# FoX scores: the second score matmul contracts 128 rows instead of 64, with the low parts of the queries repeated in both halves

## The chip, the cores and the metric

One core of one Trainium2 chip runs the whole kernel. The metric is the device time of one execution in microseconds (us); lower is better. The kernel before took 1130.22 us, the median of three runs (1130.16 to 1131.38).

## The reference, cut to what matters

One residual layer on 1024 tokens of width 1024: a normalised projection, two mixers beside each other (HGRN2 with four heads, FoX with eight heads of width 64), an output projection, a mixture of 16 experts, a final norm. The change is in FoX, which is softmax attention with a decay bias, in blocks of 128 queries:

```python
logits = jnp.einsum('bhtd,bhsd->bhts', qb, k) + (cb[..., :, None] - cum[..., None, :])
mask = (start + jnp.arange(Q_BLOCK))[:, None] >= key_pos[None, :]
logits = jnp.where(mask, logits, NEG_INF)
p = jax.nn.softmax(logits, axis=-1)
return jnp.einsum('bhts,bhsd->bhtd', p, v)
```

The inputs are float32, and the kernel keeps their accuracy by splitting a value into a high part in the type float32r and a low part, the rest.

## The kernel before, in words

The head of the kernel (about 0 to 590 us) holds the projections, HGRN2 and FoX; then come the output projection with the router (to about 740 us) and the experts. The order in which the parts are written is at lines 563 to 587: `hg_v`, `hg_fq`, `hg_core` are HGRN2, `fox_v`, `fox_gate`, `fox_kq`, `fox_core` are FoX, `hg_g` a gate projection. A planner in the build (`schedule_with_timeline_sim`) takes this order as a priority and fixes the order of each engine's instructions; each engine then runs its list strictly in order, and waits where an input is late. So attention of one pair of heads and projections or HGRN2 steps of others stand mixed in TensorE's list. The fourth pair is advanced by hand (`next(steps)`, lines 585 and 655 to 694), with pieces of the output projection (`front_a`, `front_parts`, `prep`) between its steps.

**fox_kq(p)**, line 287, makes the queries and keys of heads 2p and 2p+1. A projection (`proj_c`, lines 248 to 255, through `mm3`, lines 243 to 246: three matmuls of 128 rows and 512 columns for each of 8 slices, twice) leaves the two heads in the two halves of 128 partitions. `ev_k` and `ev_q` split it: `ka` and `kl` are the high and low parts of the keys, `qa` and `ql` those of the queries. Then copies inside the on-chip memory (`mv`, line 285, on the SP queue) arrange them: for the first head `ka` becomes high parts over low parts, and `qa` its high parts twice; `kb` and `qb` are the same for the second head. The result is a pair of operand pairs for each head.

**row(i, hh)**, line 347, makes the logits of query block i, in chunks of at most 512 keys. Each chunk is two matmuls into one PSUM bank (lines 363 and 364). The first has 128 rows: high queries twice against high and low keys. The second has 64 rows: low queries against high keys. VectorE then adds the bias and takes the minimum (lines 367 and 372), ScalarE takes the exponential (line 375). `Gt` and `Gd` are the bias tiles, made by GpSimd (lines 353 to 355). **attend** (line 378) transposes the result (line 388), splits it (lines 393, 394) and multiplies by the values (lines 398, 399); **collect** and **finish** gather the output. There are 4 pairs, 2 heads each, and 4 x 1 + 4 x 2 = 12 chunks for each head, so 96 pairs of score matmuls.

Tiles come from rotating tags: "u" (15 slots of 4 KB per partition, for all of q, k, v and the HGRN2 tiles), "L" (4 slots, for the logits of a row and others), "Gd" (3 slots). A tile that finds no free slot waits until one is released. `front_a(1)`, line 611, loads a gate tile `gm` from a pool of its own. HGRN2's score matmuls (line 491) write 64 columns of the array.

Of the kernel before, what the change touches and what calls it, by code (L numbers as in the profile page):

```python
# [7 lines left out]
F32 = mybir.dt.float32  # L8
# [11 lines left out]
NT = S // 128  # L20
# [8 lines left out]
NSLOT = E * CAP  # L29
NROW = NSLOT + NOV * 128  # L30
EPS = 1e-6
NU = 15
NWARM = 14
BIG = 1.0e30
NEG = 3.0e38
# [45 lines left out]
def build(ctx, tc, x, attn_norm, w_in, hg_lb_logits, hg_norm, fox_f_bias, fox_norm, w_out, ffn_norm,  # L81
          w_group, b_group, w_expert, b_expert, w_gate, w_up, w_down, final_norm, cf, ci, cl0, out, dbg=None):
# [8 lines left out]
    cst = ctx.enter_context(tc.tile_pool(name="cst", bufs=1))  # L91
# [56 lines left out]
    up = up_cm.__enter__()  # L148
# [6 lines left out]
    def rtile(name):  # L155
        return up.tile([128, S], F32R, name=name, tag="u", bufs=NU)

    def ltile(name):
        return up.tile([128, S], F32, name=name, tag="L", bufs=4)
# [18 lines left out]
        return hi, lo  # L178

    XT, HV0 = [], []  # L180
    xst = cst.tile([128, NT, 5], F32, name="xst")
    warm = ltile("warm")[:, 0:128]
    V.memset(warm, 0.0)
    b = rbank()
# [99 lines left out]
    def mv(d, o):  # L284
        nc.sync.dma_start(d.bitcast(F32), o.bitcast(F32))

    def fox_kq(p):
        ka, kb, qa, qb, ql = (rtile(n) for n in ("ka", "kb", "qa", "qb", "ql"))
        kl = up.tile([128, S], F32R, name="kl", tag="L", bufs=4)

        def ev_k(b, sl):
            A.copy(ka[:, sl], b)
            V.tensor_sub(kl[:, sl], b, ka[:, sl].bitcast(F32))  # L293

        def ev_q(b, sl):
            A.activation(qa[:, sl], b, AF.Copy, scale=-0.125)
            V.scalar_tensor_tensor(ql[:, sl], b, -0.125, qa[:, sl].bitcast(F32), op0=OP.mult, op1=OP.subtract)
        proj_c(2560 + 128 * p, ev_k)
        mv(kb[64:128], ka[64:128])
        mv(kb[0:64], kl[64:128])  # L300
        mv(ka[64:128], kl[0:64])
        proj_c(2048 + 128 * p, ev_q)
        mv(qb[64:128], qa[64:128])
        mv(qb[0:64], qa[64:128])
        mv(qa[64:128], qa[0:64])
        out = (((qa, ka), (ql[0:64], ka[0:64])), ((qb, kb), (ql[64:128], kb[64:128])))
        FS[p] = out

    cld = dr.tile([64, 128], F32, name="cld")
# [1 line left out]
    def fox_gate():  # L311
        zt = ltile("zt")[:, 0:256].rearrange("p (a b) -> p a b", a=4)
        ffv = ff.rearrange("p h i -> p (h i)")
        V.tensor_scalar(zt[:, 0], ffv, 0.0, None, op0=OP.min)
        V.scalar_tensor_tensor(zt[:, 1], ffv, -1.0, ffv, op0=OP.mult, op1=OP.max)
        A.activation(zt[:, 2], zt[:, 1], AF.Exp, scale=-1.0)
        A.activation(zt[:, 2], zt[:, 2], AF.Ln, bias=1.0)
        V.tensor_sub(zt[:, 3], zt[:, 0], zt[:, 2])
        b = cbank()
        T.matmul(b[:, 0:64], tri, zt[:, 3], start=True, stop=True)  # L320
        cl = up.tile([128, 128], F32, name="cl", tag="Gd", bufs=3)[:, 0:64]
        V.tensor_copy(cl, b[:, 0:64])
        b = cbank()
        T.transpose(b[0:64, 0:128], cl, ident)
        clT = up.tile([128, 128], F32, name="clT", tag="Gd", bufs=3)[0:64]
        V.tensor_copy(clT, b[0:64, 0:128])
        nc.sync.dma_start(cld, clT)

    cdv = cld.rearrange("r s -> (r s)")
    fls = cst.tile([128, 4, 5, 8, 2], F32, name="fls")  # L330

    LF = {}

    def fox_steps(p):
        Gt, ntot = [], []
        for hh in range(2):
            h = 2 * p + hh
# [3 lines left out]
            V.tensor_scalar(n_, g_[:, :, 127], -1.0, None, op0=OP.mult)  # L341
            Gt.append(g_)
            ntot.append(n_)
        fl = fls[:, p]
        OS = otile("OF")

        def row(i, hh):
            nb = i + 1
            (q1, k1), (q2, k2) = FS[p][hh]
            qi = slice(i * 128, (i + 1) * 128)  # L350
            gv = Gt[hh].rearrange("p i s -> p (i s)")
            Gd = up.tile([128, 128], F32, name="Gd", tag="Gd", bufs=3)
            G.tensor_add(Gd, Gt[hh][:, i], msk)
            if i:
                G.tensor_scalar(Gt[hh][:, 0:i], Gt[hh][:, 0:i], 1.0, ntot[hh][:, i - 1:i], op0=OP.mult, op1=OP.add)  # L355
            L = ltile("Lg")
            mn = up.tile([128, 4], F32, name="mn", tag="mn", bufs=6)
            prev = 3.0e38
            k = 0
            for c0 in range(0, nb * 128, 512):  # L360
                c1 = min(nb * 128, c0 + 512)
                b = rbank()
                T.matmul(b[:, :c1 - c0], q1[:, qi], k1[:, c0:c1], start=True, stop=False)
                T.matmul(b[:, :c1 - c0], q2[:, qi], k2[:, c0:c1], start=False, stop=True)
                e = min(c1, i * 128)
                if e > c0:
                    V.tensor_tensor_reduce(L[:, c0:e], b[:, :e - c0], gv[:, c0:e], scale=1.0, scalar=prev,  # L367
                                           op0=OP.add, op1=OP.min, accum_out=mn[:, k:k + 1])
                    prev = mn[:, k:k + 1]
                    k += 1  # L370
                if c1 == nb * 128:
                    V.tensor_tensor_reduce(L[:, e:c1], b[:, e - c0:c1 - c0], Gd, scale=1.0, scalar=prev,
                                           op0=OP.add, op1=OP.min, accum_out=mn[:, k:k + 1])
                    prev = mn[:, k:k + 1]
            A.activation(L[:, :nb * 128], L[:, :nb * 128], AF.Exp, scale=-1.0, bias=prev, accum_out=fl[:, 0, i, hh:hh + 1])
            return L
# [97 lines left out]
        proj_c(512 + 128 * h, ev_f)  # L474
        proj_c(128 * h, ev_q)

    hgs = cst.tile([128, 4, 4, NT], F32, name="hgs")

    def hg_core(h):
        Fh, Kh, Qh, VV = HF[h], HK[h], HQ[h], HV[h]  # L480
        sct = up.tile([128, S], F32, name="sc", tag="sc", bufs=1).rearrange("p (c t) -> p c t", c=NT)
        sc = [sct[:, 0:4], sct[:, 4:8]]

# [12 lines left out]
        for li, hs in enumerate(LEVELS):  # L496
# [8 lines left out]
            n = S // (2 * hs)  # L505
# [8 lines left out]
        for half in range(2):  # L514
            bk = hbank()
            for c in range(4):
                s_ = slice((half * 4 + c) * 128, (half * 4 + c + 1) * 128)
                T.transpose(bk[:, c * 128:(c + 1) * 128], Kh[:, s_], ident)
            kt = Kh[:, half * 512:half * 512 + 512]
            A.copy(kt, bk)  # L520
            bv = hbank()
            nn = 4 if half == 0 else 3
            for c in range(nn):
                cc = half * 4 + c
                T.matmul(bv[:, c * 128:(c + 1) * 128], kt[:, c * 128:(c + 1) * 128], VV[:, cc * 128:(cc + 1) * 128],
                         start=True, stop=True)
            for c in range(nn):
                cc = half * 4 + c
                s_ = up.tile([128, 128], F32, name="st", tag="st", bufs=4)
                if cc == 0:  # L530
                    V.tensor_copy(s_, bv[:, 0:128])
                else:
                    V.scalar_tensor_tensor(s_, st[cc], Fh[:, cc * 128 + 127:cc * 128 + 128],
                                           bv[:, c * 128:(c + 1) * 128], op0=OP.mult, op1=OP.add)
                st[cc + 1 if cc < NT - 1 else 0] = s_
            bo = hbank()
            for c in range(4):
                cc = half * 4 + c
                cs = slice(c * 128, c * 128 + 128)
                v = VV[:, cc * 128:(cc + 1) * 128]  # L540
                T.matmul(bo[:, cs], sc[half][:, c], v, start=True, stop=cc == 0)
                if cc:
                    T.matmul(bo[:, cs], Qh[:, cc * 128:(cc + 1) * 128], st[cc], start=False, stop=True)
            isl = slice(half * 4, half * 4 + 4)
            A.copy(sc[half], bo.rearrange("p (c v) -> p c v", c=4))
            sq = Qh[:, half * 512:half * 512 + 512].rearrange("p (i v) -> p i v", i=4)
            G.tensor_mul(sq, sc[half], sc[half])
            st_ = hgs[:, h, :, 4 * half:4 * half + 4]
            V.tensor_reduce(st_[:, 0], sq, axis=AX.X, op=OP.add)
            V.tensor_scalar(st_[:, 0], st_[:, 0], 1.0 / 128, EPS, op0=OP.mult, op1=OP.add)  # L550
            rsqrt(st_[:, 1], st_[:, 0], st_[:, 2], st_[:, 3])
            G.tensor_mul(sc[half], sc[half], st_[:, 1, :, None].to_broadcast([128, 4, 128]))
            nc.sync.dma_start(o_d[512 * half:512 * half + 512, 128 * h:128 * h + 128].rearrange("(i t) c -> t i c", t=128), sc[half])
# [57 lines left out]
    def front_a(i):  # L611
        om = oa.tile([128, D], F32, name="om")
        if i < 1:
            HE[i] = oa.tile([128, D], F32, name="he", bufs=1)
        gm = HE[i][:, 0:512] if i in HE else (hp[0] if hp else oa).tile([128, 512], F32, name="gm", bufs=1)
        nc.sync.dma_start(om, o_d[i * 128:(i + 1) * 128, :])
        nc.sync.dma_start(gm, g_d[i * 128:(i + 1) * 128, :])
        V.tensor_mul(om[:, 0:512], om[:, 0:512], gm)
# [708 lines left out]
```

## Time and profile before

| | |
|---|---|
| median of three runs | 1130.22 us |
| span of the profiled execution, first to last instruction | 1129.1 us (its own time is not listed apart) |
| TensorE matmul busy | 1070.2 us, 95% of the span |
| VectorE, ScalarE, GpSimd busy | 61%, 47%, 38% |
| score matmuls (lines 363 and 364) | 192, in 96 pairs, from 140 to 584 us |

Times in the trace are in us from the span's start. Matmuls are pipelined and their ends are modelled, so the distance from one start to the next is the better measure of what one costs. PE is TensorE's matmul, PEld its weight load, DVE VectorE, ACT ScalarE, POOL GpSimd, SP the engine that issues most transfers. "64\*128" in a row of PE is the shape of the loaded weights, 64 rows by 128 columns. "issue" as a releaser means that the engine waited for nothing that the profile shows.

### The profile page before, as it was taken

The page shows a single profiled execution, that of the slowest core. Times are in us where ns is not written, and L with a number is a line of the kernel's source. Part 1 is how long each engine was busy: PE and PEld are TensorE (multiplying, and loading weights), DVE is VectorE, ACT ScalarE, POOL GpSimd, SP SyncE. Part 2 cuts the span into 40 slices and gives each one's busy share as a digit, 9 for nine tenths or more (in the row PEclk, how much of TensorE's full clock was granted, in tenths as well). Part 3 has the DMA queues.
Part 4 walks back from the last instruction along what each step waited for, and adds up shares of the span by engine and source line. Part 5 has one row for each costly group of instructions (what it writes and reads, how often), then busy time and mean ns, then how long its engine had stood idle before and what let it go on. Part 6 is the DMA issues. An engine that isn't in the chain of part 4 may idle for free. (4 is left out here: it accounts for less than half of the span.)

```text
span 1129.1 us, 19387 instructions
## 1 busy us (share of the span) xinstructions
PE 1070.2 (95%) x7405; PEld 881.9 (78%) x7405; DVE 684.5 (61%) x1674; ACT 536.3 (47%) x884; POOL 428.9 (38%) x382
## 2 busy tenths in 40 slices
PE   7999999999999999889989999699999999999993
PEld 7988877788879877778967888576777778778791
DVE  5446346664677238843484576656777777778363
ACT  6423264423443264325671242465666767667241
POOL 2023244433352136422261232444655555555213
PEclk8999999999999999998999999799999999999997
DMA  7211510222111411161135952379999999999973
GB/s 240 54 42 39 141 47 19 66 66 57 39 48 44 116 38 29 48 212 68 43 117 154 397 184 94 99 242 373 370 308 319 364 325 360 318 319 376 298 262 134
DMA packets 102048, 193.98 MB, mean 172 GB/s; under 512 B 9468, under 2 KB 43372, under 8 KB 101952
## 3 DMA queue, kind: packets, MB, share of 16 engines
q1 hardware_dynamic: 90656, 169.97, 43.0%
q0 software_dynamic: 7568, 20.96, 7.5%
q10 hardware_dynamic: 3728, 1.77, 0.7%
q8 instruction: 60, 0.98, 0.4%
q14 instruction: 36, 0.29, 0.1%
HBM read 155.85 MB, written 30.68 MB: 165 GB/s over the span
## 5 line engine op out<-in xcount | busy, mean ns | idle before, releaser
L244 PE MATMUL bk<-whi,xhi 128*128 128x256 f32 (+1 forms) x384 | 113.9, 296 | 2.3 <-ACT xhi L212 1.8
L245 PE MATMUL bk<-wlo,xhi 128*128 128x256 f32 (+1 forms) x384 | 112.5, 293 | 0.7 <-DVE wlo L177 0.7
L246 PE MATMUL bk<-whi,xlo 128*128 128x256 f32 (+1 forms) x384 | 112.2, 292 | 0.0
L1029 DVE TENSOR_TENSOR wl<-we,wh 128x1024 fp32r<-128x1024 f32 x64 | 92.0, 1448 | 33.2 <-ACT wh L1027 32.2
L1027 ACT CAST wh<-wm 128x1024 fp32r<-128x1024 f32 x84 | 87.2, 1049 | 48.3 <-PE ch L246 45.4
L245 PE MATMUL ch<-wl,xh 128*128 128x512 f32 (+1 forms) x336 | 108.1, 322 | 0.0
L244 PE MATMUL ch<-wh,xh 128*128 128x512 f32 (+1 forms) x336 | 107.2, 326 | 0.0
L246 PE MATMUL ch<-wh,xl 128*128 128x512 f32 (+1 forms) x336 | 107.1, 320 | 0.0
L1027 ACT CAST wh<-we 128x1024 fp32r<-128x1024 f32 x84 | 87.2, 1049 | 38.4 <-PE ch L246 38.2
L244 PE MATMUL bk<-xhi,whi 128*128 128x512 f32 x256 | 103.2, 403 | 1.7 <-DVE kl L293 1.2
L1029 DVE TENSOR_TENSOR wl<-wm,wh 128x1024 fp32r<-128x1024 f32 x63 | 93.5, 1515 | 17.0 <-ACT wh L1027 17.0
L245 PE MATMUL bk<-xlo,whi 128*128 128x512 f32 x256 | 102.5, 400 | 0.0
L246 PE MATMUL bk<-xhi,wlo 128*128 128x512 f32 x256 | 101.6, 397 | 0.0
L355 POOL TENSOR_SCALAR Gt<-Gt,ntot 128x128 f32<-128x128 f32 (+6 forms) x56 | 44.6, 796 | 91.8 <-DVE mn L367 82.1
L393 ACT CAST ph<-ch 128x512 fp32r<-128x512 f32 (+1 forms) x80 | 42.8, 542 | 76.8 <-PE ch L388 76.7
L244 PEld LDWEIGHTS bk<-whi,xhi 128*128 128x128 f32 x384 | 75.5, 196 | 4.9 <-ACT xhi L212 2.4
L1029 POOL TENSOR_TENSOR wl<-we,wh 128x1024 fp32r<-128x1024 f32 x20 | 51.1, 2554 | 69.8 <-ACT wh L1027 69.8
L245 PEld LDWEIGHTS bk<-wlo,xhi 128*128 128x128 f32 x384 | 75.2, 196 | 2.3 <-DVE wlo L177 1.2
L246 PEld LDWEIGHTS bk<-whi,xlo 128*128 128x128 f32 x384 | 75.1, 196 | 1.6 <-issue 0.9
L1029 POOL TENSOR_TENSOR wl<-wm,wh 128x1024 fp32r<-128x1024 f32 x21 | 52.4, 2493 | 53.2 <-ACT wh L1027 53.2
L245 PEld LDWEIGHTS ch<-wl,xh 128*128 128x128 f32 x336 | 64.0, 190 | 9.0 <-issue 4.1
L244 PEld LDWEIGHTS ch<-wh,xh 128*128 128x128 f32 x336 | 63.4, 190 | 7.8 <-ACT xh L1041 1.6
(413 smaller groups left out, 2719.6 us busy)
## 6 DMA issues: line engine op xcount, KB each, us to landing
we<-in_w_gate_dram SPq DMA_DIRECT2D x8, 2048.0 KB
we<-in_w_up_dram SPq DMA_DIRECT2D x8, 2048.0 KB, 18.2
we<-in_w_down_dram SPq DMA_DIRECT2D x8, 2048.0 KB, 15.7
wm<-in_w_gate_dram SPq DMA_DIRECT2D x8, 2048.0 KB, 8.5
wm<-in_w_up_dram SPq DMA_DIRECT2D x8, 2048.0 KB
wm<-in_w_down_dram SPq DMA_DIRECT2D x8, 2048.0 KB, 14.1
wraw<-in_w_in_dram SPq DMA_DIRECT2D x26, 512.0 KB, 4.2
xt<-in_x_dram SPq DMA_DIRECT2D x8, 512.0 KB, 11.6
```

Source lines behind the costliest of these rows:

```text
L244: T.matmul(o, l[0], r[0], start=first, stop=False)
L245: T.matmul(o, l[0], r[1], start=False, stop=False)
L246: T.matmul(o, l[1], r[0], start=False, stop=last)
L355: G.tensor_scalar(Gt[hh][:, 0:i], Gt[hh][:, 0:i], 1.0, ntot[hh][:, i - 1:i], op0=OP.mult, op1=OP.add)
L393: LF['act'] = A.copy(ph[:, :o], b[:, :o])
L1027: A.copy(hi, src)
L1029: (G if j % 3 == 2 else V).tensor_sub(lo, src, hi.bitcast(F32))
```

## The change

The low parts of the queries get the layout that the high parts have. `ql` becomes the first head's low parts in both halves, and a new tile `qm` holds the second head's in both halves; three more copies make them, the third of which overwrites a part that the first two read. The second score matmul takes whole tiles, so it contracts 128 rows, and adds the product of the low queries and the low keys. Space for the new tile: "u" has 16 slots; "Gd" has 2; the small tiles `xst`, `fls`, `hgs` move into rotating tags; `gm` of `front_a(1)` takes a slot of "L".

```diff
-NU = 15
+NU = 16
...
-    xst = cst.tile([128, NT, 5], F32, name="xst")
+    xst = up.tile([128, NT, 5], F32, name="xst", tag="sg", bufs=2)
...
-        ka, kb, qa, qb, ql = (rtile(n) for n in ("ka", "kb", "qa", "qb", "ql"))
+        ka, kb, qa, qb, ql, qm = (rtile(n) for n in ("ka", "kb", "qa", "qb", "ql", "qm"))
...
         mv(qb[64:128], qa[64:128])
         mv(qb[0:64], qa[64:128])
         mv(qa[64:128], qa[0:64])
-        out = (((qa, ka), (ql[0:64], ka[0:64])), ((qb, kb), (ql[64:128], kb[64:128])))
+        mv(qm[64:128], ql[64:128])
+        mv(qm[0:64], ql[64:128])
+        mv(ql[64:128], ql[0:64])
+        out = (((qa, ka), (ql, ka)), ((qb, kb), (qm, kb)))
...
-        cl = up.tile([128, 128], F32, name="cl", tag="Gd", bufs=3)[:, 0:64]
+        cl = up.tile([128, 128], F32, name="cl", tag="Gd", bufs=2)[:, 0:64]
...
-    fls = cst.tile([128, 4, 5, 8, 2], F32, name="fls")
...
-        fl = fls[:, p]
+        fl = up.tile([128, 5, 8, 2], F32, name="fls", tag="fls", bufs=2)
...
-            Gd = up.tile([128, 128], F32, name="Gd", tag="Gd", bufs=3)
+            Gd = up.tile([128, 128], F32, name="Gd", tag="Gd", bufs=2)
...
-    hgs = cst.tile([128, 4, 4, NT], F32, name="hgs")
...
+        hgs = up.tile([128, 4, NT], F32, name="hgs", tag="hgs", bufs=2)
...
-            st_ = hgs[:, h, :, 4 * half:4 * half + 4]
+            st_ = hgs[:, :, 4 * half:4 * half + 4]
...
-        gm = HE[i][:, 0:512] if i in HE else (hp[0] if hp else oa).tile([128, 512], F32, name="gm", bufs=1)
+        gm = HE[i][:, 0:512] if i in HE else hp[0].tile([128, 512], F32, name="gm", bufs=1) if hp else ltile("gm")[:, 0:512]
```

## Rows read from the trace of the kernel before

**Rows 1.** Windows, attention stages: length; busy PE, PEld, DVE, ACT, POOL; clock; DMA share; GB/s

```profile
135.00:225.00 90.00, 89.88 (x565) 66.91 (x564) 49.79 (x143) 47.85 (x75) 38.37 (x50) 1.00 0.19 54
262.00:330.00 68.00, 67.41 (x568) 54.90 (x567) 43.82 (x142) 26.95 (x72) 28.17 (x39) 1.00 0.13 37
393.00:462.00 69.00, 66.33 (x490) 48.31 (x488) 44.00 (x125) 33.17 (x60) 33.03 (x43) 1.00 0.13 36
504.00:590.00 86.00, 78.50 (x500) 67.33 (x501) 47.11 (x137) 56.48 (x93) 32.80 (x33) 0.92 0.28 94
```

**Rows 2.** TensorE's timeline around one pair of score matmuls: start, duration, line, tiles, shape

```profile
419.62 0.40 PE L363 MATMUL rb<-ka,qa 128*128 128x512 f32 x1
419.95 0.50 PE L364 MATMUL rb<-ka,ql 64*128 64x512 f32 x1
420.38 0.50 PE L245 MATMUL bk<-xlo,whi 128*128 128x512 f32 x1
420.72 0.39 PE L246 MATMUL bk<-xhi,wlo 128*128 128x512 f32 x1
420.95 0.39 PE L244 MATMUL bk<-xhi,whi 128*128 128x512 f32 x1
```

**Rows 3.** TensorE's weight loads in the same stretch, by timeline

```profile
419.95 0.18 PEld L364 LDWEIGHTS rb<-ka,ql 64*128 64x128 f32 x1 [0.37 <-issue]
420.38 0.19 PEld L245 LDWEIGHTS bk<-xlo,whi 128*128 128x128 f32 x1 [0.25 <-issue]
...
420.72 0.19 PEld L244 LDWEIGHTS bk<-xhi,whi 128*128 128x128 f32 x1
```

**Rows 4.** TensorE's timeline at smaller widths, and at the lines 491 and 388

```profile
262.40 0.28 PE L245 MATMUL bk<-wlo,xhi 128*128 128x256 f32 x1
262.52 0.28 PE L246 MATMUL bk<-whi,xlo 128*128 128x256 f32 x1
262.73 0.34 PE L491 MATMUL hc<-hQ,hK 128*64 128x64 f32 x4
...
147.33 0.38 PE L364 MATMUL rb<-kb,ql 64*128 64x256 f32 x1
147.64 0.44 PE L388 MATMUL ch<-cft,Lg 128*128 128x128 f32 x2
147.83 0.48 PE L244 MATMUL bk<-xhi,whi 128*128 128x512 f32 x1
```

**Rows 5.** SP's issues of query copies of pairs 0 to 2, and output weights, by timeline

```profile
132.58 2.08 SPq L285 DMA_DIRECT2D qb<-qa  x2
134.76 0.53 SPq L172 DMA_DIRECT2D wraw<-in_w_in_dram  x1
137.55 0.46 SPq L285 DMA_DIRECT2D qa<-qa  x1
...
261.31 0.47 SPq L285 DMA_DIRECT2D qa<-qa  x1
...
389.97 0.46 SPq L285 DMA_DIRECT2D qa<-qa  x1
...
493.37 2.51 SPq L592 DMA_DIRECT2D woraw<-in_w_out_dram  x3
```

**Rows 6.** Time from issue to landing of the copies into qb, by tile

```profile
DMA to landing us min/median/max: 2.9/3.6/3.7
```

**Rows 7.** TensorE's timeline: the first L364 of pairs 0, 1 and 2

```profile
140.91 0.32 PE L364 MATMUL rb<-ka,ql 64*128 64x128 f32 x1
...
264.55 0.33 PE L364 MATMUL rb<-ka,ql 64*128 64x128 f32 x1
...
395.68 0.33 PE L364 MATMUL rb<-ka,ql 64*128 64x128 f32 x1
```

**Rows 8.** Waits of the fourth attention stage: who, for whom, total us, times, longest

```profile
PE bk L624 <- DVE om L618: 1.8, 1, 1.8
PE rb L363 <- DMA qa<-qa: 1.7, 1, 1.7
```

More of the change, by code (lines that the diff above doesn't have):

```diff
@@ L324, in fox_gate @@
         T.transpose(b[0:64, 0:128], cl, ident)
-        clT = up.tile([128, 128], F32, name="clT", tag="Gd", bufs=3)[0:64]
+        clT = up.tile([128, 128], F32, name="clT", tag="Gd", bufs=2)[0:64]
         V.tensor_copy(clT, b[0:64, 0:128])
```

## The prediction

> **What bounds the kernel now.** I read three views. First the windows over the four stretches in which attention runs [rows 1]: TensorE is busy for 89.88 of 90 us, 67.41 of 68, 66.33 of 69 and 78.50 of 86, while VectorE, the next, has 49.79 of 90 and 47.11 of 86. So TensorE sets the pace in the first two stages, nearly so in the third, and in the fourth most of the time. A busy TensorE can still be held up inside, so the second view is its timeline, read by distances between starts [rows 2]. Ordinary matmuls of 512 columns stand 0.23 us apart (420.72 to 420.95). Around a 64-row score matmul the distances are 0.33 (419.62 to 419.95), 0.43 (to 420.38) and 0.34 us (to 420.72). Three ordinary ones would take 0.70 us; these take 1.10. The third view, the weight loads [rows 3], says why: in the ordinary stream a load starts while the matmul before it runs (L244's load at 420.72, its matmul at 420.95). The load of the 64-row matmul starts only together with that matmul, after 0.37 us without a load, and the load of the 128-row matmul behind it is late too (0.25 us). Going from 128 rows to 64 and back stops the loading ahead, twice for each pair.
>
> **Part 1, the wider matmul.** The same 96 matmuls remain, with the same columns and the same weight columns; only the rows grow. An L364 of 128 rows has the form of L363, so I price it as an ordinary member of the stream. The saving has three distances, taken from [rows 2]:
> - from the matmul before to L364: 0.33 less 0.23, 0.10 us, for all 96: 9.6 us;
> - from L364 to the next: 0.43 less 0.23, 0.20 us. Eleven of the 96 are followed by L491, which writes 64 columns and brings a hold-up of its own: L246 of 256 columns is followed after 0.21 us by L491, against 0.12 us in the stream [rows 4]. That half stays. So 85 x 0.20 + 11 x 0.10 = 18.1 us;
> - from that matmul to its successor: 0.34 less 0.23, 0.11 us. It is absent where transposes follow, which take 0.19 us for two [rows 4]: 21 cases, and I leave out the 11 with L491. So 64 x 0.11 = 7.0 us.
>
> Narrower chunks (half of the 96) lose about the same: 256 columns take 0.31 us to the next start [rows 4] against 0.12 in the stream, 0.19 us. The sum is **34.7 us of TensorE**, 8.7 us in each stage.
>
> What the page says against it: the Trainium skill, TensorE: Matmul & The Clock Gate, Part 3, states that a weight load overlaps a running matmul only when their row groups differ. By it a 128-row matmul among 128-row matmuls could not load ahead, and this saving would be nil. Rows 3 speak against it here: L244's load starts 0.23 us before its own matmul, under one that uses the same 128 rows.
>
> **How much reaches the end.** In stages one and two TensorE hardly idles, so I count 0.9 of 8.7 us in each; VectorE and GpSimd, at about 55% and 43% there, leave room. The third idles for 2.7 us and the fourth for 7.5 us of waits on the row chain, which a quicker TensorE meets sooner: 0.8 and 0.6. What is late next is the softmax chain of one row (VectorE, ScalarE, then transposes). Together 3.2 x 8.7 = **27.8 us** kept.
>
> **Part 2, three more copies for each pair.** VectorE has written ql well before; the cost is the wait of the first L364 of a pair, which used ql directly and now waits for the last copy, and everything queued on TensorE behind it. SP issues its list in order, at about 0.5 us each, and a copy lands 2.9 to 3.7 us after its issue [rows 5, 6]. The third copy waits for the two into qm, as the copy into qa waits for those into qb. If the planner puts the qm copies right behind the qb copies (they are ready then), they are out by about 135.7 us, landed by 139.3, and ql is complete at 142.2 us, against a first L364 at 140.91 [rows 7]: 1.3 us lost for pair 0. That is 4.65 us after the issue into qa at 137.55; by the same count pair 1 loses 1.4 us (261.31 + 4.65 against 264.55) and pair 2 nothing (389.97 + 4.65 against 395.68). If they stand behind qa, two issues, two landings and an issue between come to about 8 us after it: 4.6, 4.8 and 2.3 us. In pair 3, loads of the output weights stand in the same list [rows 5], and L363 already waited 1.7 us for qa [rows 8]; a second trip through that queue costs, by an estimate from these rows, between 0.5 (an issue) and 5 us (three loads' issues and a landing). The ends are 3 and 17 us. I take the first order and about the middle for pair 3, 1.3 + 1.4 + 0 + 3 = **5.7 us**, since the planner moves ready copies forward, as it did with a weight load ahead of qa [rows 5]. The next projection's weights, issued behind these copies on SP, are covered by a projection of 48 matmuls in flight (11 us); without that cover they cost the same wait once more, inside the upper end. The bytes, 256 KB for each copy, go to transfer engines that are 13 to 28% busy [rows 1].
>
> **Part 3, tiles.** The sixth tile of a pair takes the sixteenth slot, so with one pair live nothing changes: no gain, no loss. gm in an L slot holds back one of four row buffers while front_a(1) loads and must first wait for a row to be released; the nearest row is the 1.8 us for which L624 waited on such a tile [rows 8]. Between 0 and 4 us, I take 1.5. Gd with two slots makes GpSimd wait one row earlier for VectorE; GpSimd is the least busy of the four in that stage (32.80 of 86 us) and can lose time without holding TensorE. Between 0 and 3 us, I take 0.5. The moved small tiles are written afresh and have two slots; nothing waits for them in a stage's length. Together **2.0 us**.
>
> **Sum.** The profiled span is 1129.1 us; the median of the runs is 1.1 us above it, which I leave unchanged. 1130.2 - 27.8 + 5.7 + 2.0 = 1110.1, so **1110 us**.
>
> **Rivals.**
> - *The copies hold TensorE.* ql's copies stand late in SP's list, at the upper ends: 27.8 - 17 - 2 = 9 us saved, 1121 us. For it: an in-order queue, and a wait already seen for qa [rows 8]. Against: the planner knows of the copies and can place L364 later, with projections ahead of it.
> - *The row chain takes over.* TensorE runs into VectorE and ScalarE, and only half is kept: 17.4 - 7.7 = 10 us saved, 1120 us. For it: the idle time of stages three and four. Against: almost none in the others.
> - *Slower: the mixture of work breaks up.* With two pairs live, they need 12 of 16 "u" slots, where it was 10 of 15, so 4 are left for HGRN2 tiles instead of 5, and a projection that should fill attention's gaps waits until attention ends. The place is the join of one pair with the next; the price is that of the fourth stage, which lacks filler: 7.5 us idle, and a granted clock of 0.92, that is 16% of it at 1.2 instead of 2.4 GHz, worth 6.9 us; 14.4 us for a stage [rows 1]. One such stage leaves a gain of 5.7 us; from two on it decides: 28.8 against 20.1, 1139 us. Against: the first two stages, with 15 slots, have no idle time to speak of, so their filler is ample, and one slot in five has to be the one that matters twice.
> - *The change does not do what it says.* Loading ahead stays blocked for another reason than the change of rows, and the distances stay at 0.43. Then only the costs remain: 1130.2 + 7.7, 1138 us. The rows speak against it: L363, of 128 rows and the same keys, loads ahead where it follows 128 rows. The page's rule above would give this same time.
>
> **How the numbers follow.** My forecast has 0.68, with its own range of 1098 (nearly all 34.7 kept, copies hidden) to 1118; the copies 0.11, the row chain 0.09, the broken mixture 0.08, the unchanged distances 0.04. The range 1098 to 1126 takes in the first three cases. A measurement of this kernel tells about 0.2%, 2.3 us, from no change. Faster 0.87, same 0.04 (the two middle rivals at their worst, or one broken stage with late copies), slower 0.09.
>
> **What would show it.** Right: L364 as 128\*128, its load starting before its matmul, and distances of about 0.23 us at 512 columns behind and ahead; each stage about 7 us shorter (the fourth 5). Copies: waits of L364 for a DMA into ql, at most 1 to 3 us for a pair. Wrong: distances of 0.43 us unchanged; or distances gone and TensorE idle in front of L388, L398 or L363 for VectorE and ScalarE; or stages with a clock below 1.00 that had 1.00.

## The result, and the profile after

The changed kernel takes 1117.55 us (median of four runs, 1116.34 to 1119.09) against 1130.8 us for the kernel before in the same session: a ratio of 0.9876, with a 95% interval of 0.986 to 0.9892, or 14 us less by the ratio. The forecast was 20 us less, 1110 us, with a range of 1098 to 1126. The result lies in the range, 7.5 us above the forecast.

In the changed kernel the numbers of the lines behind line 306 grow by two or three: L363 and L364 are now L365 and L366, L388 is L390, L399 is L401, L491 is L493, L618 and L624 are L620 and L626.

The page of the changed kernel, TensorE's busy time first: 1038.1 us, where it was 1070.2.

```profile
span 1117.3 us, 19427 instructions
...
PE 1038.1 (93%) x7405; PEld 875.8 (78%) x7405; DVE 682.6 (61%) x1674; ACT 539.2 (48%) x886; POOL 427.8 (38%) x382
```

TensorE lost 32.1 us of busy time and the span 11.8, so 20 us of the gain have turned into idle time. First, where the busy time went. TensorE's timeline of the changed kernel around one pair of score matmuls, and its weight loads (columns as in [rows 2, 3]):

```profile
168.31 0.39 PE L246 MATMUL bk<-xhi,wlo 128*128 128x512 f32 x1
168.54 0.40 PE L365 MATMUL rb<-ka,qa 128*128 128x512 f32 x1
168.77 0.40 PE L366 MATMUL rb<-ka,ql 128*128 128x512 f32 x1
169.00 0.40 PE L244 MATMUL bk<-xhi,whi 128*128 128x512 f32 x1
169.24 0.39 PE L245 MATMUL bk<-xlo,whi 128*128 128x512 f32 x1
...
168.54 0.19 PEld L366 LDWEIGHTS rb<-ka,ql 128*128 128x128 f32 x1
```

All distances between starts are 0.23 to 0.24 us, where they were 0.33, 0.43 and 0.34 [rows 2]. The load of the score matmul now starts at 168.54, 0.23 us ahead of its matmul, under L365; it used to start together with it [rows 3].

Second, where it stayed. The windows of the four attention stages, each from the first score matmul of a pair of heads until its last one starts, first in the kernel before, then in the changed kernel (columns as in [rows 1]):

```profile
140.65:220.70 80.05, 80.05 (x506) 58.95 (x506) 46.11 (x133) 44.98 (x70) 35.23 (x46) 1.00 0.14 40
264.40:328.50 64.10, 63.51 (x535) 51.74 (x533) 41.19 (x130) 26.51 (x70) 28.17 (x39) 1.00 0.12 34
395.53:459.90 64.37, 62.91 (x477) 45.91 (x475) 41.93 (x119) 31.51 (x57) 30.93 (x42) 1.00 0.14 38
504.92:584.00 79.08, 73.11 (x469) 63.05 (x469) 42.38 (x127) 51.62 (x85) 29.19 (x32) 0.91 0.29 98
```

```profile
145.11:222.10 76.99, 75.46 (x506) 60.58 (x507) 46.23 (x133) 43.31 (x68) 34.85 (x47) 0.96 0.16 45
268.12:330.10 61.98, 57.12 (x578) 51.28 (x579) 43.40 (x126) 26.19 (x67) 30.45 (x44) 1.00 0.14 39
392.56:456.70 64.14, 56.38 (x499) 46.55 (x498) 45.93 (x127) 31.99 (x59) 36.42 (x48) 1.00 0.15 43
496.74:568.70 71.96, 62.34 (x462) 57.09 (x462) 41.21 (x123) 52.38 (x84) 29.10 (x33) 0.98 0.36 121
```

The length of a window less TensorE's busy time, the first two numbers, is its idle time: 0.0, 0.6, 1.5 and 6.0 us before, 1.5, 4.9, 7.8 and 9.6 after. The stages hold different numbers of matmuls here, since the planner made a new order for the whole kernel; the experiments give pairs of kernels that can be subtracted. Two things are new. The first score matmul of pair 0 (the first two heads) starts at 145.11 us, where it was 140.65, and the first stage has a granted clock of 0.96 where it had 1.00.

The waits of TensorE in the first stage of the changed kernel (who, for whom, total us, times, longest); there were none of this kind before:

```profile
PE rb L365 <- DMA qa<-qa: 3.4, 1, 3.4
PE rb L366 <- DMA ql<-ql: 1.5, 1, 1.5
```

and in the fourth (496.74 to 568.70 us), where [rows 8] had 1.8 for om and 1.7 for qa:

```profile
PE bk L626 <- DVE om L620: 3.1, 1, 3.1
PE ub L401 <- DVE pl L396: 2.5, 3, 1.5
...
PE rb L365 <- DMA qa<-qa: 1.9, 1, 1.9
PE rb L366 <- DMA ql<-ql: 0.8, 1, 0.8
```

### The profile page after: what moved, and what is told of

It reads as the page before. It is cut to its first block, busy times and chain, and to the rows that moved or that the text cites. A ratio compares the mean times of both kernels' runs of the same rounds, so it can differ in the third digit from the quotient of the medians.

```text
span 1117.3 us, 19427 instructions
## 1 busy us (share of the span) xinstructions
PE 1038.1 (93%) x7405; PEld 875.8 (78%) x7405; DVE 682.6 (61%) x1674; ACT 539.2 (48%) x886; POOL 427.8 (38%) x382
## 5 line engine op out<-in xcount | busy, mean ns | idle before, releaser
L377 ACT ACTIVATE Lg<-Lg,mn 128x128 f32<-128x128 f32 (+3 forms) x64 | 49.7, 777 | 41.7 <-DVE mn L374 40.6
```

## The experiments

Each kernel was timed beside the kernel before; "gain" is the ratio's distance from 1 times 1131 us. Since the planner makes a new order for every kernel, a difference between two of them holds some microseconds of order as well. One measure of that: from the last matmul of the output projection to the end of the span the programs are the same, but this takes 414.1 us before, 414.6 in the changed kernel, 416.9 in copies64 and 418.2 in rows_only. It goes with TensorE's granted clock: in the first 45 us of that part its mean is 0.85, 0.85, 0.77 and 0.73.

| kernel | what it has | median us | ratio, 95% interval | gain us |
|---|---|---|---|---|
| the changed kernel | 128 rows, copies, tile edits | 1117.55 | 0.9876 [0.986, 0.9892] | 14.0 |
| rows_only | 128 rows | 1111.93 | 0.9816 [0.9796, 0.9836] | 20.8 |
| copies64 | copies, tile edits | 1138.11 | 1.0045 [1.0024, 1.0066] | -5.1 |
| tiles_only | tile edits | 1139.97 | 1.0057 [1.0033, 1.008] | -6.4 |
| both64 | both score matmuls 64 rows | 1133.5 | 1.0003 [0.9986, 1.0021] | -0.3 |
| rows_tiles | 128 rows, tile edits | 1117.12 | 0.9871 [0.9851, 0.9891] | 14.6 |
| rows_copies | 128 rows, copies, 15 slots | 1127.87 | 0.9959 [0.9941, 0.9976] | 4.6 |
| zero_halves | as changed, zeros for copies | 1112.73 | 0.983 [0.981, 0.9851] | 19.2 |
| zero_dummy | zero_halves, idle transfers | 1115.71 | 0.9851 [0.9826, 0.9876] | 16.9 |
| rows_gm | 128 rows, gm in L | 1117.9 | 0.9867 [0.9842, 0.9893] | 15.0 |
| rows_small | 128 rows, other tile edits | 1108.02 | 0.9784 [0.9761, 0.9808] | 24.4 |
| after_sc | as changed, gm not in L | 1121.13 | 0.99 [0.9884, 0.9916] | 11.3 |
| zero_sc | zero_halves, gm not in L | 1109.5 | 0.9816 [0.9798, 0.9833] | 20.8 |

### What the rows are worth: rows_only, copies64, tiles_only

rows_only is the kernel before with one line changed:

```diff
-        out = (((qa, ka), (ql[0:64], ka[0:64])), ((qb, kb), (ql[64:128], kb[64:128])))
+        out = (((qa, ka), (ql, ka)), ((qb, kb), (ql, kb)))
```

> The kernel before with one edit: the second score matmul takes the whole tiles ql and ka (or kb), 128 rows, with no copies and no change of tiles. It adds the low queries of the other head times low keys, so the products are not the same. Theory A (the copies and the tile edits took back what is missing): TensorE busy 1036 to 1040 us as in the changed kernel, no wait for a DMA into ql, 1103 to 1111 us. Rival B (the row chain of VectorE and ScalarE takes the freed time whatever else is done): 1115 to 1119 us, the time of the changed kernel, with TensorE's waits on lines 394 and 393 as long as there.

What it adds is no product of the reference: the low queries of the other head times low keys. Measured: 20.8 us less, and 1042.9 us of TensorE. The median of 1111.93 lies just above theory A's 1103 to 1111, and the 1115 to 1119 of rival B are out. Its order is nearly that of the kernel before (all 96 pairs have the same lines around them), with the same numbers of matmuls in the four stages, so these windows can be subtracted from those of before:

```profile
141.21:213.90 72.69, 72.69 (x506) 58.46 (x507) 46.51 (x133) 44.53 (x70) 34.70 (x46) 1.00 0.15 45
257.47:314.80 57.33, 56.17 (x536) 50.76 (x534) 40.51 (x130) 26.70 (x70) 28.36 (x39) 1.00 0.14 38
381.69:442.30 60.61, 55.68 (x478) 45.44 (x476) 41.88 (x119) 31.16 (x57) 30.92 (x42) 1.00 0.15 40
486.93:562.00 75.07, 66.50 (x469) 61.29 (x470) 42.02 (x127) 51.40 (x85) 29.12 (x32) 0.91 0.29 102
```

TensorE is busy for 7.4, 7.3, 7.2 and 6.6 us less, 28.5 in sum, almost the same in each stage. The stages become shorter by 7.4, 6.8, 3.8 and 4.0 us, 21.9 in sum. The first two keep nearly all. In the third, idle time grows from 1.5 to 4.9 us, in the fourth from 6.0 to 8.6: there the saved time is not kept. The new waits of the third are short ones on several chains: 1.3 us of score matmuls for VectorE's minimum, 1.0 for pl, 0.9 for ut, and 1.3 of HGRN2's L491 for VectorE and GpSimd. In the fourth none is new; those for om, Lg, qa and pl grow by 0.4 to 0.9 us each.

copies64 is the changed kernel with its second matmul cut back to 64 rows (the diff below, against the changed kernel). tiles_only is the kernel before with all lines of the change that don't touch the score matmul, qm or the copies: NU, xst, cl, clT, fls, Gd, hgs and gm.

```diff
-        out = (((qa, ka), (ql, ka)), ((qb, kb), (qm, kb)))
+        out = (((qa, ka), (ql[0:64], ka[0:64])), ((qb, kb), (qm[64:128], kb[64:128])))
```

> The changed kernel with the second score matmul cut back to 64 rows (ql[0:64] with ka[0:64], qm[64:128] with kb[64:128]): copies and tiles are there, the 128-row matmul is not. Theory A: the copies cost 5 to 9 us and the tiles up to 4, so 1135 to 1143 us. Rival B: the costs are covered while TensorE is the bound, 1130 to 1133 us. Distances of 0.43 us after each 64-row matmul are back under every theory.

> The kernel before with the tile edits alone (16 slots of u, Gd with 2, xst, fls and hgs in rotating tags, gm in a slot of L); five query and key tiles for a pair, no copies, the second matmul with 64 rows. Theory A: 1130 to 1134 us, at most 4 us lost. Rival C (the tile edits are what ate the gain, through the order that the planner makes of them): 1136 us or more. By rival B they cost nothing, 1130 us.

Measured: 5.1 and 6.4 us more than before, by theory A for copies64 and by rival C for tiles_only (its eight runs spread from 1135.03 to 1142.88 us). From copies64 to the changed kernel, which differ in the rows alone, it is 19.1 us (1.0045 less 0.9876). copies64 runs nearly the changed kernel's order, and the pair shown above stands there too, in TensorE's timeline and loads:

```profile
168.90 0.40 PE L365 MATMUL rb<-ka,qa 128*128 128x512 f32 x1
169.23 0.49 PE L366 MATMUL rb<-ka,ql 64*128 64x512 f32 x1
169.66 0.50 PE L244 MATMUL bk<-xhi,whi 128*128 128x512 f32 x1
170.00 0.39 PE L245 MATMUL bk<-xlo,whi 128*128 128x512 f32 x1
...
169.23 0.18 PEld L366 LDWEIGHTS rb<-ka,ql 64*128 64x128 f32 x1 [0.37 <-issue]
169.66 0.19 PEld L244 LDWEIGHTS bk<-xhi,whi 128*128 128x128 f32 x1 [0.24 <-issue]
```

0.33, 0.43 and 0.34 us between the same four lines that stand 0.23 to 0.24 apart with 128 rows. So the saving is one of the rows and of nothing else in the change. By the times it is worth 19 to 21 us; up to the last matmul of the output projection, in the profiled executions, 17.0 us from copies64 to the changed kernel and 23.1 in rows_only.

### Is it the 64 rows or the change of rows: both64

Here the first score matmul has 64 rows as well, so that the two stand beside each other:

```diff
-        out = (((qa, ka), (ql[0:64], ka[0:64])), ((qb, kb), (ql[64:128], kb[64:128])))
+        out = (((qa[0:64], ka[0:64]), (ql[0:64], ka[0:64])), ((qb[64:128], kb[64:128]), (ql[64:128], kb[64:128])))
```

> The kernel before with the first score matmul cut to 64 rows too (high queries times high keys; the product with the low keys is left out), so that the two score matmuls of a chunk have the same rows. If it is the change of rows that stops the loading ahead: from the first to the second 0.23 to 0.34 us at 512 columns, and from the second to the next 128-row matmul 0.43 as before; time within 4 us of the kernel before. If a 64-row matmul is slow by itself: 0.43 us behind each of the two, 9 to 19 us more than the kernel before.

Measured: no change in time, and this timeline of TensorE:

```profile
421.84 0.39 PE L244 MATMUL bk<-xhi,whi 128*128 128x512 f32 x1
422.16 0.50 PE L363 MATMUL rb<-ka,qa 64*128 64x512 f32 x1
422.49 0.39 PE L364 MATMUL rb<-ka,ql 64*128 64x512 f32 x1
422.82 0.50 PE L245 MATMUL bk<-xlo,whi 128*128 128x512 f32 x1
423.16 0.39 PE L246 MATMUL bk<-xhi,wlo 128*128 128x512 f32 x1
...
422.26 0.19 PEld L364 LDWEIGHTS rb<-ka,ql 64*128 64x128 f32 x1
```

The distances are 0.32, 0.33, 0.33 and 0.34 us: 0.39 us over four ordinary ones of 0.23 (4 x 0.232), as much as the 0.40 that one 64-row matmul cost before. Twice as many matmuls of 64 rows cost nothing more, so what costs is going there and back, not the matmul of 64 rows. The distance behind the second was expected at 0.43 and is 0.33; the loss is spread over four distances instead of three, the sum is the same. The load of L364 starts 0.23 us ahead of its matmul here, under L363 of the same 64 rows; with L363 at 128 rows it started together with it [rows 3]. Yet L364 stands 0.33 us behind L363 and not 0.23, so a late load of its own is not the whole of what holds a matmul up at a change of rows; what the rest is, no run shows.

The Trainium skill, TensorEngine Tiling (Array Packing), Key Properties, says that changing the tiling mode drains TensorE. If going from 128 rows to 64 counts as such a change, the timeline agrees, with about 0.2 us for each way; no run here shows the drain itself.

### What the copies cost: rows_copies, zero_halves, zero_dummy

rows_copies is the kernel before with 128 rows, the three copies and the tile qm, but leaves "u" at 15 slots and the other tiles as they were.

```diff
...
+        mv(qm[64:128], ql[64:128])
+        mv(qm[0:64], ql[64:128])
+        mv(ql[64:128], ql[0:64])
...
+        out = (((qa, ka), (ql, ka)), ((qb, kb), (qm, kb)))
```

> rows_only with the three copies and the tile qm added, all other tiles as in the kernel before, 15 slots of u for six tiles a pair. If the copies cost nothing net (as the pair tiles_only and copies64 says): 1110 to 1114 us, though TensorE waits for DMA into qa and ql as it does in the changed kernel. If they cost what was forecast: 1116 to 1120 us. If the missing slot matters, above 1120 us.

Measured: 16 us slower than rows_only, far more than the copies were meant to cost. The place is the output weights. In the fourth stage the values, the pair's six tiles and the eight woraw loads need 16 slots of "u" (2 + 6 + 8). With 15, the eighth load waits for a release and is issued at 563.9 us, right behind the last score matmul of the pair's first head (563.68); in the changed kernel the last leaves at 501.7. The group of these loads in rows_copies, and then in the changed kernel (columns: line, queue, operation, tiles, count: duration ns, first and last start us):

```profile
L595 SPq DMA_DIRECT2D woraw<-in_w_out_dram x8: 328/439/882, 492.7 to 563.9; - x8
```

```profile
L594 SPq DMA_DIRECT2D woraw<-in_w_out_dram x8: 327/500/814, 491.1 to 501.7; - x8
```

The output projection starts at 585.8 us there, at 576.0 in the changed kernel and at 566.4 in rows_only. The fourth stage, up to its last score matmul, lasts 80.4 us in rows_copies and 71.9 in the changed kernel. So about 10 of these 16 us go with the missing slot; as the two kernels differ in the other tiles as well, that share is an estimate.

zero_halves therefore keeps all tiles and slots of the changed kernel and takes away only the copies. VectorE writes the low queries straight into ql[0:64] and qm[64:128], and GpSimd sets the other halves to zero. By that VectorE is busy for 692.4 instead of 682.6 us and GpSimd for 435.3 instead of 427.8:

```diff
-            V.scalar_tensor_tensor(ql[:, sl], b, -0.125, qa[:, sl].bitcast(F32), op0=OP.mult, op1=OP.subtract)
+            for t, r in ((ql, slice(0, 64)), (qm, slice(64, 128))):
+                V.scalar_tensor_tensor(t[r, sl], b[r], -0.125, qa[r, sl].bitcast(F32), op0=OP.mult, op1=OP.subtract)
...
+        G.memset(ql[64:128].bitcast(F32), 0.0)
+        G.memset(qm[0:64].bitcast(F32), 0.0)
...
-        mv(qm[64:128], ql[64:128])
-        mv(qm[0:64], ql[64:128])
-        mv(ql[64:128], ql[0:64])
```

> The changed kernel, its tiles and slots, without the three copies: VectorE writes the low queries of the two heads into a half of ql and of qm, GpSimd sets the other halves to zero, so the product of low queries and low keys is left out as in the kernel before. Theory E (the copies cost about what was forecast, and an order with more switches hid it in the pair rows_tiles and the changed kernel): no TensorE wait for DMA into ql, 1111 to 1115 us. If the copies cost nothing: 1116 to 1120 us.

Measured: 5.2 us faster than the changed kernel (0.9876 less 0.983). That is the copies' price, close to the 5.7 of the forecast (with the extra work just named on the other side of the difference). Where it lies is another matter. SP's issues of pair 0 in the changed kernel, by timeline:

```profile
134.07 2.12 SPq L285 DMA_DIRECT2D qb<-qa  x2
136.29 0.53 SPq L172 DMA_DIRECT2D wraw<-in_w_in_dram  x1
136.93 1.58 SPq L285 DMA_DIRECT2D qm<-ql  x2
139.05 0.46 SPq L285 DMA_DIRECT2D qa<-qa  x1
144.24 0.46 SPq L285 DMA_DIRECT2D ql<-ql  x1
```

The planner did put the copies into qm right behind those into qb, as the forecast took it, and the copy into qa leaves only 1.5 us later than before (139.05 against 137.55 [rows 5]; 138.89 in zero_halves). But it then takes 6.0 us to land, where it took 3.1 before and 2.9 in zero_halves. The transfer engines are full while it waits: DMA share is the last number but one in these windows from 137 to 141 us, in the changed kernel and then in zero_halves.

```profile
137.00:141.00 4.00, 4.00 (x25) 3.46 (x24) 0.00 (x0) 0.00 (x0) 1.27 (x2) 1.00 1.04 255
```

```profile
137.00:141.00 4.00, 2.88 (x21) 2.51 (x19) 0.00 (x0) 1.07 (x2) 0.00 (x0) 1.00 0.70 184
```

In zero_halves the first score matmul starts at 141.82, 3.3 us earlier than in the changed kernel:

```profile
141.82 0.33 PE L365 MATMUL rb<-ka,qa 128*128 128x128 f32 x1 [1.94 <-DMA qa<-qa]
```

A second cost follows from the wait. TensorE's timeline of the changed kernel at its first score matmuls:

```profile
145.11 0.50 PE L365 MATMUL rb<-ka,qa 128*128 128x128 f32 x2 [3.45 <-DMA qa<-qa]
147.13 0.79 PE L366 MATMUL rb<-ka,ql 128*128 128x128 f32 x2 [1.53 <-DMA ql<-ql]
147.72 0.63 PE L245 MATMUL bk<-xlo,whi 128*128 128x512 f32 x1
148.15 0.63 PE L246 MATMUL bk<-xhi,wlo 128*128 128x512 f32 x1
...
152.84 0.47 PE L245 MATMUL bk<-xlo,whi 128*128 128x512 f32 x1
153.15 0.40 PE L246 MATMUL bk<-xhi,wlo 128*128 128x512 f32 x1
```

After idling for 3.45 and 1.53 us, matmuls of 512 columns stand 0.43 us apart until 152.84, and 0.23 from 153.15 on. The window of the stretch in between has a granted clock of 0.50, the lower level (the number behind GpSimd's):

```profile
149.00:153.00 4.00, 4.00 (x11) 3.12 (x10) 1.66 (x2) 2.43 (x4) 1.85 (x4) 0.50 0.00 2
```

The twelve of them from 147.72 to 152.84 take 5.12 us instead of 12 x 0.23, so the lower clock costs 2.3 us on top of the wait. In all, pair 0's last chunk starts (L365) at 221.79 us against 214.04 in zero_halves, 7.7 us later. That is more than the 5.2 us at the end, so later parts make up for some of it.

In copies64 the first score matmul waits for qa as long (3.4 us), but no score matmul of pair 0 waits for ql, and distances of 0.43 us end at 148.98. So a part of the copies' cost shows only with the quicker rows, and makes the 19.1 us above smaller than the rows alone are worth.

Is it the traffic ahead of qa, or the wait for ql itself? zero_dummy puts the traffic back, and nobody waits for it:

```diff
+    scr = dr.tile([128, S], F32, name="scr")
...
         mv(qa[64:128], qa[0:64])
+        mv(scr[64:128], qm[64:128])
+        mv(scr[0:64], ql[0:64])
```

> The kernel zero_halves (its product of low queries and low keys is left out, as in the kernel before) with two more transfers for each pair, of 256 KB each, from the low queries to a scratch tensor that nothing reads, written behind the copy into qa where the changed kernel has its copies into qm. No matmul waits for them. Theory C (the copies cost time because, issued ahead of the copy into qa, they fill the transfer engines and make qa land late: 6.0 us after its issue in the changed kernel against 2.9 in zero_halves, and 3.1 before): if the planner again issues them ahead of qa, qa lands 5 to 6 us after its issue in pair 0, the first score matmul starts near 145 us (zero_halves 141.8, changed kernel 145.1) after a wait of 3 us or more, TensorE then runs for some us at the lower granted clock, and most of the 5 us come back: 1115.5 to 1118, ratio 0.985 to 0.989. Theory Q (the cost is that score matmuls wait for ql itself, late in the list of SP): qa lands in about 3 us, the first score matmul starts at 142 us, and the time stays at 1111 to 1114, ratio 0.982 to 0.985. If the planner issues them behind qa, both theories give about 1112.7 and the run tells nothing.

Measured: 1115.71 us, 2.4 us more than zero_halves by the ratios (their intervals overlap; the profiled spans differ by 3.2). The two transfers leave ahead of the copy into qa, as wanted (at 135.16 and 136.05 us; the weight load is pushed back by them from 134.10 to 137.45, and qa leaves at 139.21), and the events are those of theory C. TensorE's timeline (L368 is the first score matmul there), and a window behind it:

```profile
145.29 0.47 PE L368 MATMUL rb<-ka,qa 128*128 128x128 f32 x1 [4.59 <-DMA qa<-qa]
```

```profile
145.00:149.00 4.00, 3.71 (x11) 3.13 (x12) 2.00 (x8) 1.10 (x4) 2.48 (x5) 0.50 0.00 2
```

The start at 145.29, the wait of 4.59 us and the lower clock until 151 are there without any copy that the matmuls need. The time lands just inside theory C's span, at its lower end: the traffic ahead of qa accounts for about half of the copies' price. The last matmul of the output projection says the same, at 696.2 us in zero_halves, 699.6 in zero_dummy and 702.7 in the changed kernel. The other half fits the waits for ql itself, which stay out here: 1.5 us in pair 0, 0.8 in pair 1 and 0.8 in pair 3 of the changed kernel, 3.1 in sum. No run takes these waits out alone, so the second half is argued, not shown.

### What the tiles cost: rows_tiles, rows_gm, rows_small, after_sc, zero_sc

rows_tiles is rows_only with the tile edits of tiles_only; rows_gm and rows_small split them. rows_gm is rows_only with the edit of gm:

```diff
-        gm = HE[i][:, 0:512] if i in HE else (hp[0] if hp else oa).tile([128, 512], F32, name="gm", bufs=1)
+        gm = HE[i][:, 0:512] if i in HE else hp[0].tile([128, 512], F32, name="gm", bufs=1) if hp else ltile("gm")[:, 0:512]
```

> Rows of 128 with the tile edits, without copies and without qm. Theory A: the time of rows_only plus at most 4 us, 1104 to 1113 us. Rival C: 6 us or more above rows_only. Rival B: 1115 to 1119 us.

> rows_only with one tile edit, gm of front_a(1) in a slot of L. Theory G (this edit is what the tile edits cost): the load of gm is issued some 10 us later, the output projection starts about 10 us after the last score matmul instead of 4.6, and the time is 4 to 7 us above rows_only, 1116 to 1119 us beside 1112. Rival D (the loss is spread over the other edits through the planner's order): within 2 us of rows_only.

rows_small is rows_only with the other ones, NU left at 15:

```diff
-    xst = cst.tile([128, NT, 5], F32, name="xst")
+    xst = up.tile([128, NT, 5], F32, name="xst", tag="sg", bufs=2)
...
-        fl = fls[:, p]
+        fl = up.tile([128, 5, 8, 2], F32, name="fls", tag="fls", bufs=2)
...
-            Gd = up.tile([128, 128], F32, name="Gd", tag="Gd", bufs=3)
+            Gd = up.tile([128, 128], F32, name="Gd", tag="Gd", bufs=2)
...
+        hgs = up.tile([128, 4, NT], F32, name="hgs", tag="hgs", bufs=2)
```

> rows_only with the other tile edits that need no sixteenth slot: Gd with 2 slots, xst, fls and hgs in rotating tags, gm left in its own pool, 15 slots of u. Theory G: within 2 us of rows_only, 1110 to 1114 us. Rival D: 4 us or more above it.

Measured: against rows_only, rows_tiles costs 6.2 us and rows_gm 5.8, while rows_small is 3.6 us faster (their intervals overlap; neither theory had it faster). Most of this last gain comes from behind the output projection (418.2 us in rows_only, 414.3 in rows_small), so it is no merit of the small tiles, but they cost nothing. The edit of gm does. Its loads, by group, in rows_only and then in rows_gm (the first start is that of front_a(1)):

```profile
L617 SPq DMA_DIRECT2D gm<-g_d x7: 320/506/2441, 544.1 to 641.8; - x7
```

```profile
L617 SPq DMA_DIRECT2D gm<-g_d x7: 319/320/2439, 554.3 to 651.3; - x7
```

gm is asked for 10 us later. It now needs a slot of L, and SP waits there 1.4 us for L388, the transposes that read a row of logits. The last chunks of the two start at nearly the same time (L363 at 561.8 and 562.1 us), but the output projection behind them at 566.4 and 572.3.

That price doesn't carry over to the changed kernel. after_sc and zero_sc take gm out of L again and put it into a slot of HGRN2's that is free by then:

```diff
-        ... if hp else ltile("gm")[:, 0:512]
+        ... if hp else up.tile([128, S], F32, name="gm", tag="sc", bufs=1)[:, 0:512]
```

> The changed kernel with one edit: gm of front_a(1) takes the slot of the tag sc, which HGRN2 has left by then, and not one of L. Theory G (holding a slot of L is what gm costs): its load is issued some 10 us earlier, the output projection starts about 5 us after the last score matmul, 1111 to 1114 us. If the late gm is hidden behind the copies: 1116 to 1119 us.

> zero_halves with gm in the slot of the tag sc. By theories E and G together 1106 to 1110 us, the two gains added; if they cover each other 1111 to 1114 us; by neither 1116 to 1119 us.

Measured: after_sc is no faster than the changed kernel (0.99 against 0.9876, overlapping intervals), zero_sc 1.6 us faster than zero_halves, again with overlapping intervals. In after_sc gm is asked for at 533.3 us instead of 560.8 and the output projection follows 5.2 us behind the last chunk (L365) instead of 7.6; but that chunk comes 4.1 us later, at 572.5, in another order of the list. So an expectation fell: gm in L costs 5.8 us in the order of rows_only, 0 to 1.6 in those of the changed kernel and zero_halves. What in the order decides it wasn't found.

One pair of kernels misleads: rows_tiles and the changed kernel differ by the copies and take the same time, which seems to say that copies are free. But without qm a slot of "u" is spare, and the planner makes another order of it: in TensorE's instructions from 120 to 710 us there are 154 changes between L491's 64-column matmuls and others in rows_tiles, 102 in the changed kernel and 122 in the kernel before. tiles_only, with the same spare slot, has 154 too. At about 0.1 us each (0.21 against 0.12 us on the way in [rows 4]) the difference is 5 us, and TensorE's busy time is 1047.0 against 1038.1; the rest of that was not traced. Two effects of opposite sign cancel, and zero_halves has the slots right.

Of all kernels rows_small is the fastest, 24.4 us under the kernel before and about 10 under the changed one. It needs neither the copies nor qm, but like rows_only it adds a product that the reference doesn't have. zero_sc, which keeps the sums of the kernel before, is at 20.8.

## Why the prediction was right, and where it was wrong

**The mechanism was right, and sized nearly right.** Loads start ahead, and the distances are 0.23 us at 512 columns. In 83 of the 96 pairs no wait of TensorE over 0.1 us stands within the three distances, before or in rows_only; subtracting them gives 0.10, 0.17 and 0.08 us, 0.34 in sum, or 33 us for 96 pairs where the forecast had 34.7 (it took 0.10, 0.19 and 0.07 on average). The halves that were held back for L491 were rightly held back: those eleven pairs saved 0.19 us on average, the others 0.36. Transposes behind a pair did not take the third distance away, as was assumed, but left 0.06 us of it. TensorE's busy time fell by 27.3 us in rows_only and by 33.0 from copies64 to the changed kernel. The page's rule (the Trainium skill, TensorE: Matmul & The Clock Gate, Part 3, as the prediction tells it) would have left the distances at 0.43; the trace of after is against it, with a 128-row load 0.23 us ahead of its matmul under another of the same 128 rows. Part 2 of that page (Step-by-step) also lets a load go ahead into a background weight buffer; the loads ahead in these rows agree with that, though no row shows the buffer. The rival that the change doesn't do what it says falls with it.

**How much reaches the end: this step failed.** It counted 0.9, 0.9, 0.8 and 0.6 of 8.7 us in the four stages, 27.8 us. By the windows of rows_only the stages gave 7.4, 6.8, 3.8 and 4.0, 21.9 us; from copies64 to the changed kernel 4.5, 4.5, 4.4 and 4.1 in the windows, and 19.1 us by the times. How much of the miss is share and how much is size depends on the measure. Against the 33 us of the distances, rows_only kept 0.67 instead of 0.8, and 4.3 of the 5.9 us are share. Against TensorE's busy time, which fell by 28.5 us in the windows, it kept 0.77, and 5 us are size; the two sizes differ in part because thirteen pairs stand beside a wait, where a hold-up that is gone need not show as busy time. By stages that second share is 1.0, 0.92, 0.52 and 0.61. By both measures the stage that is furthest off is the third, which was to keep 0.8. A stage that idled for only 2.7 us before was taken as one that could give 7; but idle time in the trace of before says how long TensorE waits, not how much room it has until it waits. What was named as late next, the chain of one row (mn, pl and Lg), has 1.9 of some 3.8 us of added waits there, ut of the same attention 0.6 and the inputs of HGRN2's L491 the rest. So the rival in which the row chain takes over, at 1120 us with half kept, came nearer to the truth in mechanism than its chance of 0.09. One reading was wrong beside it: the next busiest engine of the fourth stage is ScalarE, 56.48 of 86 us, not VectorE [rows 1].

**The copies: right sum, wrong place.** 5.2 us against 5.7, and the sum came out so by luck. The order of issues was as forecast. The prediction let the first score matmul go at once and only L366 wait, 1.3 us in pair 0, 1.4 in pair 1 and 3 in pair 3. The larger wait is that of the first score matmul for qa, 3.4 us, because the step "transfer engines that are 13 to 28% busy" read the average of a stage: in the four microseconds that counted they were full. The third copy, counted to be issued by 139.3 us, left at 144.24, since the two into qm landed late too. The lower clock behind the wait, 2.3 us, was not foreseen, nor can it be read from a sum of waits. Pair 1 waited 0.6 us for qa and 0.8 for ql. Pair 3 lost 1.9 us to qa and 0.8 to ql, where it had lost 1.7 to qa before.

**The tiles: within their bounds in the changed kernel, outside them elsewhere.** 2.0 us were forecast. copies64 less the price of the copies leaves nothing for them; zero_halves is 1.6 us slower than rows_only, with overlapping intervals. tiles_only (6.4) and rows_gm (5.8) lie above the 4 us that bounded gm; of these only rows_gm shows gm alone, since TensorE's busy time grew by 8.3 us in tiles_only, with its spare slot. The nearest row, a wait of 1.8 us, was that of another order, and it is a wait for om, not for gm. Gd and the small tiles cost nothing, close to the 0.5 forecast.

**The rival on the slower side** had a real mechanism, a lack of "u" slots, and rows_copies shows it, at 16 us over rows_only. But it does not act where the rival put it, at the join of two pairs, and not in the changed kernel, where all eight loads of the output weights find a slot by 501.7 us.

In sum, the steps from the kernel before to rows_only (20.8 us gained), to zero_halves (1.6 lost, the tiles) and to the changed kernel (5.2 lost, the copies) give 14.0 us, where the forecast had 27.8, 2.0 and 5.7, or 20.1. Up to the last matmul of the output projection, in the profiled executions, the same steps are 23.1, 4.3 and 6.5. By either count most of the miss lies in what the rows bring to the end.

## What to carry to other kernels

A lone matmul of 64 rows among matmuls of 128 cost 0.3 to 0.4 us of TensorE here that no busy share shows; look at distances between starts, and fill up its rows without waiting for new copies, with zeros (zero_halves) or with what is at hand where the product it adds is too small to matter. When TensorE is to become faster, ask of each stage how soon the other chains would be late, since idle time before doesn't tell; and read transfer engines at the moment of the issue, not over a stage. Compare only kernels with the same slots, because the planner here turned a spare one into another order.

## What the runs showed of the hardware that was not expected

- Two matmuls of 64 rows beside each other lost 0.39 us in sum (both64), one alone among 128 rows 0.40 (the kernel before, [rows 2]).
- After TensorE had waited 3.45 and 1.53 us, the granted clock was 0.50 until about 153 us, 1.2 instead of 2.4 GHz, and matmuls of 512 columns stood 0.43 us apart. The same in zero_dummy after 4.59 us, until 151 us, and in copies64 after 3.42 us, until 149 us. After the wait of 1.94 us in zero_halves, they stood 0.23 us apart at once.
- The copy of 256 KB into qa of pair 0 took 6.0 us to land behind two other copies and a weight load in the changed kernel, 2.9 to 3.1 without the two (zero_halves, the kernel before).
